# Another order of the product groups inside a planned block of an f32 encoder layer

## The chip, the cores and the metric

The kernel runs on one core of a Trainium2 chip. The metric is the time of the device in microseconds; the time before is the median of 3 runs. Matmuls run on TensorE (PE in the profile); the other engines are VectorE (DVE), ScalarE (ACT), GpSimd (POOL) and SyncE (SP), which only issues transfers here.

## The reference

One encoder layer on 256 tokens of width 2048, all in f32: a SwiGLU block, an attention mixer, a second SwiGLU block, and a gated embedding at the end, each between RMS norms. The change touches the two SwiGLU blocks only (width of the hidden layer 5632):

```python
def _swiglu(u, w_gate, w_up, w_down):
    return (jax.nn.silu(u @ w_gate) * (u @ w_up)) @ w_down

f = _swiglu(_rmsnorm(h, ffn1_pre_g[i]), ffn1_w_gate[i], ffn1_w_up[i], ffn1_w_down[i])
h = h + 0.5 * _rmsnorm(f, ffn1_post_g[i])
```

## The kernel before

**A product in three matmuls.** An f32 product is made from parts. Each operand is split into a high part, rounded to the matmul's fp32r type, and a low part, the rest: for a weight tile of two 128-row groups, `split` casts on ScalarE (line 77, `wh`) and subtracts on VectorE (line 78, `wl`). `mac` then issues three matmuls for each row group: high by high (line 104), low activations by high weights (105), high activations by low weights (106). `wh` and `wl` have 6 buffers each, so splits run at most six tiles ahead of TensorE.

**Planned blocks.** The hidden layer is worked on in 11 blocks of 512 columns for each SwiGLU. Block 0 is computed plainly. Blocks 1 to 10 of each go through `pair_product`, 20 in all, which makes the gate and up products of one block with fewer matmuls by a scheme like Strassen's. The activations of 12 of the 16 row groups form a 2 by 2 matrix (two token halves, two sets of six row groups); `s1` to `s4` are sums of its parts, made once. The weights form `ra1` and `ra2` (gate) and `rb1` and `rb2` (up), of six row groups each. `rb1` never has a tile of its own: it is added into `ra1`, and later into `rb2`, by DMAs that accumulate (`add_rows`, line 195, issued by GpSimd, in three parts of two row groups each). In between VectorE adds `rb2` into `ra1` (`add`, line 204). So each of these tiles is split, then changed in place, then split again. The products are called by their left side: a11 on the plain `ra1`; s4 on the plain `rb2`; s1 on `ra1`+`rb1`; s2 on that with `rb2` added; s3 on `rb2`+`rb1`; a12 on `ra2`; a22 on `ra1` with `ra2` added. They accumulate in four PSUM banks g0, g1, u0 and u1. ScalarE copies three of the states aside (`kept`, line 175), and VectorE combines them (line 206).

**What else lies in a block.** The last 4 of the 16 row groups aren't part of the scheme: `rest_b` multiplies two of them of the up weights with both token halves (12 matmuls, into u1 and u0), and a like step does the gate weights at the end of the block. `fill` takes one job of a list: a down step, which multiplies the previous block's hidden values with 4 row groups of the down weights (24 matmuls, line 449 on), four for each block. `run_later` transposes the previous block's hidden values and splits them into `hid_h` and `hid_l` (lines 295, 301 and 302); the down steps need them. Block 1 has `rest_first` set: its rest rows of up come at the start. In the last block two entries of the list are empty, so only two down steps lie within it.

**Order.** The loads of rest rows and down weights (`raw`, line 68, three buffers) and of `ra1`, `rb2`, `ra2` (`raw_b`, line 190, three buffers) stand in one queue on SyncE. The program is built ahead of time with the Tile layer, which sets each engine's queue and its waits from a plan; a queue is then worked through in order. In the trace TensorE's is in the order of the program, and VectorE's and ScalarE's are nearly so: where two instructions were ready at different times in the plan, they can be exchanged.

The order of TensorE's work in a block before, where `rest_first` is not set: a11, s4, transposes, s1, rest 0, down 0, s2, down 1, s3, rest 1, down 2, a12, a22, down 3, and two rest steps of gate.

Of the kernel before, what the change touches and what calls it, by code (L numbers as in the profile page):

```python
# [34 lines left out]
def encoder_layer(ctx: ExitStack, tc: tile.TileContext, a: dict, out: bass.AP):  # L35
# [35 lines left out]
    def split(raw):  # L71

        n, m = raw.shape[1:]
        wh = wpool.tile([P, 2, NB], F32R, name="wh", bufs=6)[:, :, :m]
        wl = wpool.tile([P, 2, NB], F32R, name="wl", bufs=6)[:, :, :m]
        splits[:] = [
            nc.scalar.copy(wh[:, :n], raw),  # L77
            nc.vector.tensor_tensor(wl[:, :n], raw, wh[:, :n].bitcast(F32), op=ALU.subtract),  # L78
        ]
        return [(wh[:, i], wl[:, i]) for i in range(n)]  # L80

    def load_parts(w, r0, nk, c0):

        parts = []
        for k0 in range(0, nk, 4):
            n = min(4, nk - k0)
            raw = load_rows(w, r0 + k0 * P, n, c0)
            for j in range(0, n, 2):
                parts += split(raw[:, j : min(j + 2, n)])
        return parts  # L90

    def mac(acc, xs, parts, first=False, last=False, low_last=False):


        if low_last:
            for i, ((xh, xl), (wh, wl)) in enumerate(zip(xs, parts)):
                nc.tensor.matmul(acc, xh, wh, start=first and i == 0, stop=False)
                nc.tensor.matmul(acc, xh, wl, start=False, stop=False)
            for i, ((xh, xl), (wh, wl)) in enumerate(zip(xs, parts)):
                nc.tensor.matmul(acc, xl, wh, start=False, stop=last and i == len(parts) - 1)  # L100
            return
        for i, ((xh, xl), (wh, wl)) in enumerate(zip(xs, parts)):
            lead, tail = first and i == 0, last and i == len(parts) - 1
            nc.tensor.matmul(acc, xh, wh, start=lead, stop=False, skip_group_check=True)  # L104
            nc.tensor.matmul(acc, xl, wh, start=False, stop=False, skip_group_check=True)  # L105
            nc.tensor.matmul(acc, xh, wl, start=False, stop=tail, skip_group_check=True)  # L106

    def of_tile(lhs, t):
        tok = slice(t * P, (t + 1) * P)
        return [(hi[:, tok], lo[:, tok]) for hi, lo in lhs]  # L110
# [48 lines left out]
    def run_later():  # L159
        for job in later:  # L160
            job()
        later.clear()

    def pair_product(lhs, sums, wa, ca, wb, cb, fill, rest_first):

        rows1, rows2 = ([lhs[k] for k in ks] for ks in ROWS)
        a11, a12, a22 = of_tile(rows1, 0), of_tile(rows2, 0), of_tile(rows2, 1)
        s1, s2, s3, s4 = sums

        def bank(name):  # L170
            return ps_acc.tile([P, NB], F32, name=f"pair_{name}", tag="acc")

        def kept(name, x):
            t = ffn_pool[0].tile([P, NB], F32, name=name, tag="part", bufs=3)
            nc.scalar.copy(t, x)
            return t

        def spans(j, step):
            for k0, k1 in ((0, KB), (KB, RQ)):
                for k in range(k0, k1, step):  # L180
                    yield k, min(k + step, k1)

        def weight_rows(w, j, c, k0, k1):
            r0 = ROWS[j][k0] * P
            return w[r0 : r0 + (k1 - k0) * P, c : c + NB].rearrange("(k p) n -> p k n", p=P)

        def blocks(w, j, c):
            raw = ffn_pool[0].tile([P, RQ, NB], F32, name="raw_b", bufs=3)
            for k0, k1 in spans(j, KB):
                raw_loads.append(nc.sync.dma_start(raw[:, k0:k1], weight_rows(w, j, c, k0, k1)))  # L190
            return raw

        def add_rows(raw, w, j, c):
            for k0, k1 in spans(j, 2):
                nc.gpsimd.dma_start(raw[:, k0:k1], weight_rows(w, j, c, k0, k1), accum_op=ALU.add)  # L195

        def split_rows(raw):
            return sum((split(raw[:, k : min(k + 2, RQ)]) for k in range(0, RQ, 2)), [])

        def add(out_, x, y, op=ALU.add):  # L200
            n = x.shape[1] if len(x.shape) > 2 else 0
            for k in range(0, n, 2):
                j = slice(k, min(k + 2, n))
                nc.vector.tensor_tensor(out_[:, j], x[:, j], y[:, j], op=op)  # L204
            if not n:
                nc.vector.tensor_tensor(out_, x, y, op=op)

        nk = len(lhs)
        k_rest = [(k, (nk - 2 * RQ) // 2) for k in range(2 * RQ, nk, (nk - 2 * RQ) // 2)]

        def rest(w, k, n, c, accs_, last=False):
            parts = load_parts(w, k * P, n, c)
            for t, acc, lead in accs_:
                mac(acc, of_tile(lhs[k : k + n], t), parts, first=lead, last=last)

        def rest_b(i, last):
            rest(wb, *k_rest[i], cb, [(1, u1, i == 0), (0, u0, i == 0 and rest_first)], last=last)

        u0 = u1 = None
        if rest_first:  # L220
            u0, u1 = bank("u0"), bank("u1")
            rest_b(0, False)
            run_later()
        ra1, rb2 = blocks(wa, 0, ca), blocks(wb, 1, cb)
        if rest_first:
            rest_b(1, False)
        g1 = bank("g1")
        mac(g1, a11, split_rows(ra1), first=True, last=True)
        g0_ = kept("g0_s", g1)
        add_rows(ra1, wb, 0, cb)  # L230
        u0 = u0 or bank("u0")
        mac(u0, s4, split_rows(rb2), first=not rest_first, last=rest_first)
        run_later()
        if rest_first:
            fill()
        g0 = bank("g0")
        mac(g0, s1, split_rows(ra1), first=True, last=True)
        u1_ = kept("u1_s", g0)
        add(ra1, ra1, rb2)
        add_rows(rb2, wb, 0, cb)  # L240
        if not rest_first:
            u1 = bank("u1")
            rest_b(0, False)
        fill()
        mac(g1, s2, split_rows(ra1), last=True)
        u0_ = kept("u0_s", g1)
        add(u0_, u0_, u1_, ALU.subtract)
        ra2 = blocks(wa, 1, ca)
        fill()
        mac(g1, s3, split_rows(rb2), last=True)  # L250
        if not rest_first:
            rest_b(1, True)
        add(u0_, u0, u0_, ALU.subtract)
        add(u1_, u1_, g1, ALU.subtract)
        add(u1_, u1, u1_)
        if not rest_first:
            fill()
        mac(g0, a12, split_rows(ra2), first=True)
        add(ra1, ra1, ra2)
        mac(g1, a22, split_rows(ra1))  # L260
        fill()
        for k, n in k_rest:
            rest(wa, k, n, ca, [(0, g0, False), (1, g1, False)], last=k + n == nk)
        assert len(k_rest) == 2
        add(g0_, g0, g0_)
        return (g0_, g1), (u0_, u1_)
# [159 lines left out]
    def swiglu(pool, f, ssf, res, blocks, rs, sums, w_gate, w_up, w_down, g_post):  # L426
# [35 lines left out]
        for nb in range(nbs):  # L462
            c0 = nb * NB
            if True:
                if nb > 0:
                    gate, up = pair_product(lhs, sums, w_gate, c0, w_up, c0, fill, nb == 1)
                    gs = [gated(gate[t], t) for t in range(NT)]
                else:
# [396 lines left out]
```

## Time and profile before

| | |
|---|---|
| median of 3 runs | 1961.44 us (1957.82 to 1962.08) |
| the profiled execution's own time | 1963.99 us |
| its span | 1962.2 us |
| mean granted TensorE clock | 0.994 |
| TensorE busy | 1914.2 us, 98% of the span |
| VectorE busy | 1552.7 us, 79% |
| ScalarE busy | 1119.0 us, 57% |
| read from memory | 404.79 MB, 207 GB/s over the span |

The span goes from the first to the last instruction; the time is some 2 us more. Matmuls overlap in the profile: one is shown as 0.39 us, but one starts about every 0.23 us. In a timeline row stand the start in us, the duration, the engine, the line, the operation, the tile written and the tiles read, and in brackets how long the engine was idle just before and what ended that. `raw` and `raw_b` are the weight tiles as loaded, `pair_g` and `pair_u` the banks g and u, `u_h` and `u_l` the parts of the activations, `sums_h` and `sums_l` those of s1 to s4. With several alike in a row, the start is that of the first and the duration that of all.

### The profile page before, as it was taken

To read this page: it belongs to the slowest core of one execution; us is meant where nothing else is said; L and a number is where in the kernel's file an instruction comes from. 1 tells how busy PE (TensorE), PEld (TensorE's weight loads), DVE (VectorE), ACT (ScalarE), POOL (GpSimd) and SP (SyncE) were. 2 spreads that over 40 slices of the span, in tenths; PEclk is the share of its full clock that TensorE was granted. 3 is DMA by queue.
4 is the path that set the end of the run, shared out by engine and by line. 5 is a ranking of instruction groups with operands and counts; after the bars stand their busy time and mean duration, and the time that the engine had idled before them with its cause. 6 is when DMAs were issued, how large, how long until landed. Compare 5 with 4: busy or idle time off the path is not lost.

```text
span 1962.2 us, 23327 instructions
## 1 busy us (share of the span) xinstructions
PE 1914.2 (98%) x8600; PEld 1565.5 (80%) x8600; DVE 1552.7 (79%) x1740; ACT 1119.0 (57%) x1364; POOL 173.0 (9%) x151
## 2 busy tenths in 40 slices
PE   8999999999999999999999999999999999999997
PEld 6878877787778878888888888778777877888786
DVE  7888898889888986566665588778988898889864
ACT  7665565656555654554544466555655565555653
POOL 0111001100110000000000010110011001100000
PEclk9999999999999999999999999999999999999999
DMA  9887878787877647454454578778687878776463
GB/s 348 242 226 205 259 201 223 201 261 203 228 198 242 180 154 245 153 174 155 146 194 164 179 252 226 206 185 261 204 222 196 249 206 221 203 232 183 151 235 113
DMA packets 207361, 408.40 MB, mean 208 GB/s; under 512 B 8848, under 2 KB 11920, under 8 KB 206736
## 3 DMA queue, kind: packets, MB, share of 16 engines
q1 hardware_dynamic: 174608, 344.00, 51.1%
q0 software_dynamic: 32640, 62.92, 18.2%
q8 instruction: 67, 1.10, 0.2%
q14 instruction: 46, 0.38, 0.1%
HBM read 404.79 MB, written 2.10 MB: 207 GB/s over the span
## 4 chain that ended last, share of the span: by engine, by line
PE 76%; DMA 8%; DVE 8%; issue 4%; ACT 2%; POOL 2%; POOLq 0%; DVEq 0%; ACTq 0%; SPq 0%
DMA raw_b<-in_ffn_w_up 8%; PE pair_g L105 7%; PE pair_g L104 7%; PE down L105 7%; PE pair_g L106 7%; PE down L104 7%; PE down L106 7%; DVE wl L78 3%; PE pair_u L106 3%; DVE raw_b L204 2%; PE pair_u L105 2%; PE pair_u L104 2%; ACT wh L77 2%; POOL raw_b L195 2%; PE v L106 1%
## 5 line engine op out<-in xcount | busy, mean ns | idle before, releaser
L77 ACT CAST wh<-raw 128x1024 fp32r<-128x1024 f32 (+1 forms) x453 | 469.1, 1051 | 374.2 <-PE down L105 104.6
L78 DVE TENSOR_TENSOR wl<-raw,wh 128x1024 fp32r<-128x1024 f32 (+1 forms) x453 | 543.9, 1218 | 140.2 <-ACT wh L77 126.8
L77 ACT CAST wh<-raw_b 128x1024 fp32r<-128x1024 f32 x420 | 436.5, 1050 | 334.6 <-PE down L105 130.5
L78 DVE TENSOR_TENSOR wl<-raw_b,wh 128x1024 fp32r<-128x1024 f32 x420 | 505.0, 1220 | 145.5 <-ACT wh L77 138.9
L105 PE MATMUL down<-wh,hid_l 128*128 128x512 f32 x640 | 252.7, 395 | 0.0
L104 PE MATMUL down<-wh,hid_h 128*128 128x512 f32 x640 | 251.8, 393 | 0.0
L106 PE MATMUL down<-wl,hid_h 128*128 128x512 f32 x640 | 249.8, 390 | 0.0
L195 POOL DMA_DIRECT2D raw_b<-in_ffn_w_up x120 | 146.8, 1267 | 1081.5 <-DVE wl L78 772.9
L106 PE MATMUL pair_g<-wl,u_h 128*128 128x512 f32 x520 | 202.3, 389 | 0.0
L105 PE MATMUL pair_g<-wh,u_l 128*128 128x512 f32 x520 | 202.3, 389 | 0.0
L104 PE MATMUL pair_g<-wh,u_h 128*128 128x512 f32 x520 | 202.3, 389 | 0.0
L104 PEld LDWEIGHTS down<-wh,hid_h 128*128 128x128 f32 x640 | 120.7, 189 | 28.1
L104 PE MATMUL pair_g<-wh,sums_h 128*128 128x512 f32 x360 | 143.1, 397 | 0.0
L204 DVE TENSOR_TENSOR raw_b<-raw_b 128x1024 f32<-128x1024 f32 x120 | 142.7, 1217 | 0.1
L106 PEld LDWEIGHTS down<-wl,hid_h 128*128 128x128 f32 x640 | 120.6, 188 | 27.0
L105 PE MATMUL pair_g<-wh,sums_l 128*128 128x512 f32 x360 | 141.7, 394 | 0.0
L106 PE MATMUL pair_g<-wl,sums_h 128*128 128x512 f32 x360 | 141.3, 393 | 0.0
L105 PEld LDWEIGHTS down<-wh,hid_l 128*128 128x128 f32 x640 | 120.8, 189 | 25.0
L441 DVE TENSOR_TENSOR f<-f,down 128x512 f32<-128x512 f32 x160 | 108.9, 680 | 19.0 <-PE down L106 18.1
L104 PEld LDWEIGHTS pair_g<-wh,u_h 128*128 128x128 f32 x520 | 97.6, 188 | 20.4
L105 PEld LDWEIGHTS pair_g<-wh,u_l 128*128 128x128 f32 x520 | 97.6, 188 | 20.3
L106 PEld LDWEIGHTS pair_g<-wl,u_h 128*128 128x128 f32 x520 | 97.6, 188 | 20.2
(218 smaller groups left out, 2956.8 us busy)
## 6 DMA issues: line engine op xcount, KB each, us to landing
raw<-in_ffn_w_down SPq DMA_DIRECT2D x88, 1024.0 KB, 7.4
raw_b<-in_ffn_w_up POOLq DMA_DIRECT2D x120, 512.0 KB, 10.2
raw<-in_w_qkv SPq DMA_DIRECT2D x48, 1024.0 KB, 5.1
raw_b<-in_ffn_w_gate SPq DMA_DIRECT2D x40, 1024.0 KB, 5.2
raw<-in_ffn_w_gate SPq DMA_DIRECT2D x41, 512.0 KB, 5.2
raw<-in_ffn_w_up SPq DMA_DIRECT2D x40, 512.0 KB, 6.0
raw_b<-in_ffn_w_gate SPq DMA_DIRECT2D x40, 512.0 KB, 7.9
raw_b<-in_ffn_w_up SPq DMA_DIRECT2D x20, 1024.0 KB, 5.2
```

The costliest lines, as they stand in the source:

```text
L77: nc.scalar.copy(wh[:, :n], raw),
L78: nc.vector.tensor_tensor(wl[:, :n], raw, wh[:, :n].bitcast(F32), op=ALU.subtract),
L104: nc.tensor.matmul(acc, xh, wh, start=lead, stop=False, skip_group_check=True)
L105: nc.tensor.matmul(acc, xl, wh, start=False, stop=False, skip_group_check=True)
L106: nc.tensor.matmul(acc, xh, wl, start=False, stop=tail, skip_group_check=True)
L195: nc.gpsimd.dma_start(raw[:, k0:k1], weight_rows(w, j, c, k0, k1), accum_op=ALU.add)
L204: nc.vector.tensor_tensor(out_[:, j], x[:, j], y[:, j], op=op)
L441: nc.vector.tensor_tensor(f_t, f_t, acc, op=ALU.add)
```

## The change

The groups of a block are put in another order; no instruction is added or taken out. Where `rest_first` is not set, the new order of TensorE's work is: a11, s4, transposes, rest 0, down 0, s1, rest 1, down 1, s2, down 2, s3, a12, a22, down 3, and the two rest steps of gate. So a rest step and a down step now stand between s4 and s1, another pair between s1 and s2, one down step between s2 and s3, and nothing between s3 and a12. Where `rest_first` is set, the second rest step moves from the front of the block to the place between s4 and the first down step. The `stop` marks of the accumulations move with their last matmul.

```diff
         ra1, rb2 = blocks(wa, 0, ca), blocks(wb, 1, cb)
-        if rest_first:
-            rest_b(1, False)
         g1 = bank("g1")
         mac(g1, a11, split_rows(ra1), first=True, last=True)
         g0_ = kept("g0_s", g1)
         add_rows(ra1, wb, 0, cb)
         u0 = u0 or bank("u0")
-        mac(u0, s4, split_rows(rb2), first=not rest_first, last=rest_first)
+        mac(u0, s4, split_rows(rb2), first=not rest_first)
         run_later()
-        if rest_first:
-            fill()
+        if not rest_first:
+            u1 = bank("u1")
+        rest_b(int(rest_first), rest_first)
+        fill()
         g0 = bank("g0")
         mac(g0, s1, split_rows(ra1), first=True, last=True)
         u1_ = kept("u1_s", g0)
         add(ra1, ra1, rb2)
         add_rows(rb2, wb, 0, cb)
         if not rest_first:
-            u1 = bank("u1")
-            rest_b(0, False)
+            rest_b(1, True)
         fill()
         mac(g1, s2, split_rows(ra1), last=True)
         u0_ = kept("u0_s", g1)
...
         ra2 = blocks(wa, 1, ca)
         fill()
         mac(g1, s3, split_rows(rb2), last=True)
-        if not rest_first:
-            rest_b(1, True)
         add(u0_, u0, u0_, ALU.subtract)
         add(u1_, u1_, g1, ALU.subtract)
         add(u1_, u1, u1_)
-        if not rest_first:
-            fill()
         mac(g0, a12, split_rows(ra2), first=True)
         add(ra1, ra1, ra2)
         mac(g1, a22, split_rows(ra1))
```

## The prediction

> **What bounds the kernel now.** I read the page's head, then TensorE's waits, then one steady block (374.64 to 438.80 us, the fifth planned block of the first FFN) engine by engine.
>
> ```profile
> span 1962.2 us, 23327 instructions
> ...
> PE 1914.2 (98%) x8600; PEld 1565.5 (80%) x8600; DVE 1552.7 (79%) x1740; ACT 1119.0 (57%) x1364; POOL 173.0 (9%) x151
> ...
> L77 ACT CAST wh<-raw_b 128x1024 fp32r<-128x1024 f32 x420 | 436.5, 1050 | 334.6 <-PE down L105 130.5
> ```
>
> ```profile
> PE pair_u L106 <- DVE wl L78: 25.1, 18, 2.9
> ```
>
> ```profile
> 374.64:438.80 64.16, 62.74 (x279) 51.44 (x278) 55.62 (x57) 37.55 (x40) 7.34 (x6) 1.00 0.77 218
> 129.00:140.00 11.00, 8.87 (x33) 7.10 (x33) 10.75 (x11) 4.22 (x6) 1.86 (x2) 0.84 1.07 228
> 1250.00:1262.00 12.00, 9.50 (x29) 7.64 (x30) 10.60 (x12) 4.28 (x6) 2.20 (x2) 0.72 1.05 230
> 1512.00:1520.00 8.00, 6.00 (x20) 4.66 (x20) 8.00 (x9) 3.77 (x5) 1.84 (x2) 0.79 1.06 200
> 360.00:381.00 21.00, 21.00 (x94) 17.32 (x93) 15.63 (x16) 11.19 (x12) 3.62 (x3) 1.00 0.98 271
> ```
>
> TensorE sets the end: it is busy 98% of the span. Of its idle time one line holds more than half, 25.1 us in 18 waits, and 18 is the number of planned blocks that are not rest_first (nine in each of two FFNs). The steady block (window columns: length; then busy time of PE, PEld, DVE, ACT, POOL; granted clock; DMA share; GB/s) is 64.16 long with 62.74 of matmul: 1.42 idle, which is this one wait. So only about 1.4 us in a block can be won by any order of work; more can easily be lost.
>
> ```profile
> 374.64 0.39 PE L104 MATMUL pair_g<-wh,u_h 128*128 128x512 f32 x1
> 378.72 0.39 PE L104 MATMUL pair_u<-wh,sums_h 128*128 128x512 f32 x1
> 382.85 1.04 PE L295 MATMUL tr<-ident,u_s 128*128 128x128 f32 x8
> 383.64 0.48 PE L104 MATMUL pair_g<-wh,sums_h 128*128 128x512 f32 x1
> 387.86 0.40 PE L104 MATMUL pair_u<-wh,u_h 128*128 128x512 f32 x1
> 389.91 0.50 PE L106 MATMUL pair_u<-wl,u_h 128*128 128x512 f32 x1 [1.42 <-DVE wl L78]
> 392.31 0.39 PE L104 MATMUL down<-wh,hid_h 128*128 128x512 f32 x1
> 397.80 0.39 PE L104 MATMUL pair_g<-wh,sums_h 128*128 128x512 f32 x1
> ```
>
> ```profile
> 381.81 1.05 ACT L77 CAST wh<-raw_b 128x1024 fp32r<-128x1024 f32 x1 [1.86 <-DMA raw_b<-in_ffn_w_up]
> 383.24 2.96 ACT L77 CAST wh<-raw 128x1024 fp32r<-128x1024 f32 x3
> 386.09 1.07 ACT L301 CAST hid_h<-tr 128x512 fp32r<-128x512 f32 x2
> ```
>
> ```profile
> 382.89 1.23 DVE L78 TENSOR_TENSOR wl<-raw_b,wh 128x1024 fp32r<-128x1024 f32 x1 [1.68 <-ACT wh L77]
> 384.04 3.49 DVE L204 TENSOR_TENSOR raw_b<-raw_b 128x1024 f32<-128x1024 f32 x3
> 387.44 1.28 DVE L302 TENSOR_TENSOR hid_l<-tr,hid_h 128x512 fp32r<-128x512 f32 x2
> 388.64 3.48 DVE L78 TENSOR_TENSOR wl<-raw,wh 128x1024 fp32r<-128x1024 f32 x3
> ...
> 412.07 0.68 DVE L206 TENSOR_TENSOR u_s<-u_s,pair_g 128x512 f32<-128x512 f32 x1
> ```
>
> ```profile
> 365.04 2.57 POOL L195 DMA_DIRECT2D raw_b<-in_ffn_w_up  x2 [39.71 <-DVE wl L78]
> 370.52 1.20 POOL L195 DMA_DIRECT2D raw_b<-in_ffn_w_up  x1 [2.91 <-DVE wl L78]
> 385.90 3.71 POOL L195 DMA_DIRECT2D raw_b<-in_ffn_w_up  x3 [14.18 <-DVE raw_b L204]
> ```
>
> Read backwards from 389.91. TensorE lacks the low split of the first rest rows; VectorE starts it only at 388.64, behind the last split of the summed ra1 (382.89), three adds (384.04) and the hidden splits (387.44). That queue is late because ScalarE stood until 381.81 for the last accumulating DMA into ra1, issued at 370.52: 11.3 us under way, while the DMA engines were 0.98 busy. So the wait at the rest rows is the landing of the sum, handed on through two in-order queues.
>
> **The change part by part.** Times as +x from the block's first matmul at 374.64. Nothing is added or removed: per block 12 matmuls, one split and one load for each rest step, 24 matmuls, two splits and one load for each down step, all with another neighbour. TensorE's distances are unchanged: six rows 378.72-374.64 = 4.08, down 397.80-392.31 = 5.49, a rest step 12 matmuls at down's 5.49/24 = 0.229, so 2.75 where nothing waits.
>
> *The sum gets cover.* New order: a11 +0, s4 +4.1, transposes +8.2, rest +9.0, down +11.8, s1 from +17.2 instead of +9.0. The landing at 381.81 is +7.2. The six wh buffers let the cast of s1's third tile start only when s4's third is released, about +8.2 to +8.4 (the page's row shows such releases by L105), so ScalarE no longer waits for the DMA. The rest tile is now sixth after a11's first: cast about +2, needed at +9. The wait of 25.1 us goes: **-25.1**.
>
> *The clock.* The three windows with 0.84, 0.72 and 0.79 each begin at one of the longest waits:
>
> ```profile
> 131.17 0.50 PE L106 MATMUL pair_u<-wl,u_h 128*128 128x512 f32 x1 [2.13 <-DVE wl L78]
> ...
> 132.22 0.63 PE L104 MATMUL pair_u<-wh,u_h 128*128 128x512 f32 x1
> ```
>
> ```profile
> 1252.50 0.80 PE L106 MATMUL pair_u<-wl,u_h 128*128 128x512 f32 x1 [2.93 <-DVE wl L78]
> ```
>
> ```profile
> 1514.14 0.50 PE L106 MATMUL pair_u<-wl,u_h 128*128 128x512 f32 x1 [2.00 <-DVE wl L78]
> ```
>
> Matmuls of 0.63 follow where 0.39 is usual, 1.05 us after the first of these waits has ended. The loss is 0.16 x 11 + 0.28 x 12 + 0.21 x 8 = 1.8 + 3.4 + 1.7 = 6.8 us. I take it as a consequence of the waits: **-6.8** (bounds 0 and -6.8). [...]
>
> *The hidden splits lose theirs.* This is the price. Transposes to first down matmul is 9.5 us now, 3.5 then. ScalarE: s1's third cast about +8.4 to +9.45, then hid_h (two of 0.55), the first half by +10.0. VectorE then needs 0.68 for that half of hid_l: ready at +10.7 if it is free, +11.9 if it has just begun a 1.22 us split or add. The second down matmul, which reads it, starts at +11.98. Estimate 0; bounds 0 to +0.5 a block (one split and one add ahead), 0 to +9 in all. Before, the three adds ran ahead of hid_l because they could start at 384.04 and hid_h came only at 386.09, behind three casts of raw (383.24); in the new order hid_h is ready about when s1's last low split is, and hid_l stands ahead of the adds in the program.
>
> *Loads, SP's queue.* Three raw buffers, so three loads run ahead:
>
> ```profile
> 361.94 0.37 SPq L68 DMA_DIRECT2D raw<-in_ffn_w_down  x1
> ...
> 363.30 0.37 SPq L68 DMA_DIRECT2D raw<-in_ffn_w_down  x1
> 389.92 0.37 SPq L68 DMA_DIRECT2D raw<-in_ffn_w_up  x1
> ...
> raw<-in_ffn_w_down SPq DMA_DIRECT2D x88, 1024.0 KB, 7.4
> ```
>
> The third place (363.30, 1 MB for down 1) goes to the second rest rows, half as large; 0.52 MB at 271 GB/s is 1.9 us less in front of the accumulation. Down 1's load moves from 363.30 to the release of the first rest tile, about +5; with 7.4 us it lands at +12.4, its cast is allowed at +15.9, its matmuls come at +24. Covered, 0; if the cover failed, TensorE still has 8 us. The ra2 load stands after one more raw load in the program; it waits for a buffer anyway. Value 0.
>
> *The second sum.* The adds into ra1 end about +15.3 (now +12.9), so POOL's three issues (385.90, +11.3 now) come about 3 us later and land by about +31; s3's matmuls start at +39. 0. POOL has nothing else queued in the block.
>
> *The end of the block.* Before, rest and down lay between s3 and a12, so the subtraction that reads g1 (412.07, about 0.5 us after s3's end) had 12.3 us until a22 writes g1; now it has a12's 4.1. It needs 0.68 and at most one 1.22 ahead: 0.
>
> *The rest_first block.* Its second rest step moves behind s4, so a11 comes 2.7 us sooner.
>
> ```profile
> 58.15 5.77 DVE L78 TENSOR_TENSOR wl<-raw_b,wh 128x1024 fp32r<-128x1024 f32 x5
> ...
> 59.06 0.39 PE L104 MATMUL pair_g<-wh,u_h 128*128 128x512 f32 x1
> ```
>
> In the first FFN a11's second low split ends about 59.3; TensorE would want it at 56.3 + 1.4 + 0.5 = 58.1. **+1.2**; bounds 0 to +2.7 for each of two blocks, since that queue may also move.
>
> *Sum*, against the profiled execution's 1963.99: 1963.99 - 25.1 - 6.8 + 1.2 = 1933.3. That execution is 2.55 us above the median of the runs, 1961.44; the half-rate stretches can differ between executions, and if all that difference is theirs the median loses only 4.3 of them and comes out the same. Forecast 1933.
>
> **The rivals.** [...]
>
> (b) *Part of the gain goes into a wait at the first down step*: hid_l comes with a split and an add ahead, or hid_h behind a late DMA. 0.3 to 1.0 us in 18 blocks: +5 to +18, so 1938 to 1951. For it: a margin of 0.1 to 1.3 us against in-order queues, and VectorE is 55.62 of 64.16 busy. Against: 0.68 is short and comes early in program order.
>
> (c) *Slower*: VectorE's queue keeps today's order, three adds (3.49) before hid_l. Its first half is then ready at 9.5 + 1.2 + 3.4 + 0.65 = +14.75 against +11.98: 2.75 x 18 = 50, and waits as long as these keep the half-rate stretches: 1933 + 50 + 7 = 1990. It decides from 1.75 us a block (31.9/18) on. For it: it is today's order. Against: today the adds are ready first, then they are not.
>
> (d) *No change*: the wait only moves to another split, because VectorE, not the landing, is the limit: 1961. Against: 8.5 us of VectorE idle in the block, and the new order gives each split more lead.
>
> **How the numbers follow.** Forecast 0.62, (a) 0.09, (b) 0.15, (c) 0.09, (d) 0.05. No change means within 0.2%, about 4 us, roughly what runs of this kernel differ by. Faster: 0.62 + 0.09 + 0.15 = 0.86; same 0.05; slower 0.09. The likeliest case has 1929 to 1938 (0 to +5.4 at rest_first, a few us of clock). The range adds (a) and (b): 1928 to 1951, leaving out (c) and (d), 0.14, and a little at the lower end.
>
> **What would show it.** Right: no pair_u L106 line among TensorE's waits; ScalarE's waits for the accumulating DMA near zero; block length near 62.7; granted clock 1.00 in every block; in VectorE's queue hid_l ahead of the adds. Wrong: a wait of TensorE at down L104 or L105 for hid (b, c); half-rate matmuls in blocks without waits (a); a new wait at s2 or s3 for wl, which would break the cover worked out for the sums; a wait before a22 for the subtraction; a wait above 2.7 us in a rest_first block.

## The result and the profile after

The changed kernel takes 1928.08 us (median of 5 runs, 1927.68 to 1928.54) against 1961.44 us for the kernel before (median of 5, 1957.82 to 1966.69): a ratio of 0.9831 with a 95% interval of 0.9813 to 0.9849. The forecast was 1933 with a range of 1928 to 1951. The profiled execution took 1928.43 us, 35.6 less than the profiled one of before.

The head of the page, then TensorE's longest waits, then what was left of ScalarE's waits for the accumulating DMA (in us in total, times, longest):

```profile
span 1926.7 us, 23362 instructions
...
PE 1902.8 (99%) x8600; PEld 1562.8 (81%) x8600; DVE 1554.7 (81%) x1740; ACT 1128.8 (59%) x1364; POOL 172.4 (9%) x151
```

```profile
PE gate L104 <- ACT wh L77: 6.1, 2, 5.7
PE q L97 <- ACT u_h L296: 2.2, 1, 2.2
```

```profile
ACT wh L77 <- DMA raw_b<-in_ffn_w_up: 2.9, 1, 2.9
```

The pair_u line with 25.1 us is gone, and nothing has taken its place; before, the like line of ScalarE stood at 60.4 us in 40 waits:

```profile
ACT wh L77 <- DMA raw_b<-in_ffn_w_up: 60.4, 40, 3.6
```

The same block as in the prediction, now from 365.78 us, as a window (length; busy PE, PEld, DVE, ACT, POOL; clock; DMA share; GB/s) and then as its timeline on TensorE, ScalarE, VectorE and GpSimd:

```profile
365.78:428.26 62.48, 62.48 (x280) 51.53 (x278) 55.85 (x57) 38.04 (x41) 7.31 (x6) 1.00 0.80 227
```

```profile
365.78 0.39 PE L104 MATMUL pair_g<-wh,u_h 128*128 128x512 f32 x1
...
373.99 1.04 PE L290 MATMUL tr<-ident,u_s 128*128 128x128 f32 x8
374.79 0.48 PE L104 MATMUL pair_u<-wh,u_h 128*128 128x512 f32 x1
...
377.60 0.39 PE L104 MATMUL down<-wh,hid_h 128*128 128x512 f32 x1
377.83 0.39 PE L105 MATMUL down<-wh,hid_l 128*128 128x512 f32 x1
...
383.10 0.39 PE L104 MATMUL pair_g<-wh,sums_h 128*128 128x512 f32 x1
```

```profile
373.96 1.05 ACT L77 CAST wh<-raw_b 128x1024 fp32r<-128x1024 f32 x1 [0.32 <-DVE wl L78]
374.91 1.07 ACT L296 CAST hid_h<-tr 128x512 fp32r<-128x512 f32 x2
```

```profile
374.98 1.22 DVE L204 TENSOR_TENSOR raw_b<-raw_b 128x1024 f32<-128x1024 f32 x1
376.12 1.28 DVE L297 TENSOR_TENSOR hid_l<-tr,hid_h 128x512 fp32r<-128x512 f32 x2
377.32 1.22 DVE L78 TENSOR_TENSOR wl<-raw_b,wh 128x1024 fp32r<-128x1024 f32 x1
378.45 2.36 DVE L204 TENSOR_TENSOR raw_b<-raw_b 128x1024 f32<-128x1024 f32 x2
```

```profile
361.66 1.20 POOL L195 DMA_DIRECT2D raw_b<-in_ffn_w_up  x1 [2.90 <-DVE wl L78]
```

TensorE is busy through the whole block: 62.48 of 62.48, where it was 62.74 of 64.16. The third accumulating DMA is issued at -4.1 as before, and lands 9.1 us later, at +4.9, where it was 11.2 us and +7.1; s1 now starts at +17.3. ScalarE casts the third tile of the sum at +8.2 without a wait for a DMA, and VectorE makes hid_l at +10.3, behind one of the three adds and ahead of the other two. TensorE needs its first half by +12.05 (377.83).

### The profile page after: what moved, and what is told of

The parts are those of the page before. It is cut to its first block, busy times and chain, and to the rows that moved or that the text cites. A ratio compares the mean times of both kernels' runs of the same rounds, so it can differ in the third digit from the quotient of the medians.

```text
span 1926.7 us, 23362 instructions
## 1 busy us (share of the span) xinstructions
PE 1902.8 (99%) x8600; PEld 1562.8 (81%) x8600; DVE 1554.7 (81%) x1740; ACT 1128.8 (59%) x1364; POOL 172.4 (9%) x151
## 3 DMA queue, kind: packets, MB, share of 16 engines
HBM read 404.79 MB, written 2.10 MB: 211 GB/s over the span
## 4 chain that ended last, share of the span: by engine, by line
PE 95%; DVE 2%; ACT 1%; issue 1%; DMA 1%; POOL 0%; SPq 0%; DVEq 0%; POOLq 0%; ACTq 0%
PE pair_g L105 10%; PE pair_g L104 10%; PE pair_g L106 10%; PE down L105 8%; PE down L104 8%; PE down L106 8%; PE pair_u L104 3%; PE pair_u L105 3%; PE pair_u L106 3%; PE v L106 2%; PE v L105 2%; PE v L104 2%; PE mo L106 1%; PE mo L104 1%; PE mo L105 1%; PE tr L290 1%
## 5 line engine op out<-in xcount | busy, mean ns | idle before, releaser
L104 PE MATMUL down<-wh,hid_h 128*128 128x512 f32 x640 | 251.3, 393 | 0.0
L104 PE MATMUL pair_g<-wh,u_h 128*128 128x512 f32 x520 | 202.5, 389 | 0.0
L104 PEld LDWEIGHTS down<-wh,hid_h 128*128 128x128 f32 x640 | 120.2, 188 | 27.9
L104 PE MATMUL pair_g<-wh,sums_h 128*128 128x512 f32 x360 | 141.7, 394 | 0.0
L104 PEld LDWEIGHTS pair_g<-wh,u_h 128*128 128x128 f32 x520 | 97.6, 188 | 20.4
```

## The experiments

Ratios are to the kernel before, run beside each variant on the same chip; intervals are 95%.

**Without the first sum.** Is the landing of the sum the cause at all?

```diff
-        add_rows(ra1, wb, 0, cb)
```

> The order of before; the three accumulating DMAs into ra1 are left out, so the products s1 and s2 lack rb1's share. Theory (the landing of that sum is the cause, handed on through two queues): ScalarE has nothing to wait for, VectorE's queue runs about 3 us earlier at the rest rows, the 18 waits of TensorE go, and with them the half-rate stretches in the blocks: 1927 to 1931 us. Rival (VectorE's own work is the limit): the low split of the rest rows stays behind three adds and the hidden splits, the waits stay at 1 us or more in a block: 1950 to 1961.

Measured: 1928.42 us, ratio 0.9841 (0.9822 to 0.9859). TensorE's order is still that of before, yet the time is that of the changed kernel. VectorE's work is the same, so it isn't the limit, and rival (d) falls. The run also reads 31 MB less (373.33 for 404.79), so by itself it doesn't tell the landing from the traffic; the next run, which keeps the traffic, does.

**The rest step alone.**

```diff
         if rest_first:
             fill()
+        else:
+            u1 = bank("u1")
+            rest_b(0, False)
         g0 = bank("g0")
...
-        if not rest_first:
-            u1 = bank("u1")
-            rest_b(0, False)
         fill()
```

> Only the first rest step moves ahead of s1; the down step stays behind s1. Theory: s1 then starts at +11.8 instead of +9.0 and the next raw tile whose low split TensorE needs is down 0's, at +16.4; VectorE's queue (last split of the sum to about +9.6, three adds to +13.0, hidden to +14.2, down 0's first low split to +15.4) is just in time: no wait above 0.3 us in a block, 1928 to 1934 us. Rival (both steps are needed as cover): a wait of 0.5 to 1.4 us in a block at down 0, 1940 to 1958.

Measured: 1931.16 us (four runs, 1930.33 to 1938.98), ratio 0.9869 (0.9839 to 0.9899). Some 2.75 us of other matmuls ahead of s1 are cover enough in a steady block. The sum lands at +7.1 in this trace as in that of before (medians over 16 blocks, the second to the ninth planned one of each FFN, counted from a11's first matmul), so it is the cover that takes the waits away, not an earlier landing. The waits that it has and the changed kernel hasn't (0.35, 0.72 and 0.26 us) are in the last block of each FFN (see the next but one).

**The down step alone.**

```diff
-        if rest_first:
-            fill()
+        fill()
         g0 = bank("g0")
...
-        fill()
+        if rest_first:
+            fill()
         mac(g1, s2, split_rows(ra1), last=True)
```

> Only the first down step moves ahead of s1; the rest step stays behind s1. The sum has cover (s1 at +14.5). Theory: the price is the hidden values: the first down step comes straight after the transposes, whose first half ends near +8.7; hid_h and hid_l need 0.55 + 0.68 and places in two queues, so TensorE waits 1.0 to 2.2 us (and loses about 0.25 more) for hid in each of 18 blocks: 1950 to 1975 us with some half-rate stretches. Rival (hid was never tight, either step covers alike): 1928 to 1932.

Measured: 1938.21 us, ratio 0.9892 (0.9873 to 0.9910): slower than the change by 10 us, but less than the theory had it. There is no wait for hid; instead a steady block of the first FFN is 62.8 us long, 0.3 more than the 62.48 of the change (see the late transposes below). The rest is in the last block of each FFN: four waits of 0.7 to 1.0 us and a half-rate stretch (granted clock 0.79 from 1756 to 1764 us).

**The first pair alone**, with the second half of the block as before.

```diff
-        if rest_first:
-            fill()
+        if not rest_first:
+            u1 = bank("u1")
+            rest_b(0, False)
+        fill()
         g0 = bank("g0")
...
-        if not rest_first:
-            u1 = bank("u1")
-            rest_b(0, False)
-        fill()
+        if rest_first:
+            fill()
         mac(g1, s2, split_rows(ra1), last=True)
```

> Rest 0 and down 0 move ahead of s1 as in the change; s2 then follows s1 directly, and the second half of the block (down 1, s3, rest 1, down 2) stays as before. Theory: the gain is in the first pair alone; the adds are done before s2's casts are allowed, and the second sum lands some 4 us before s3 needs it: no wait, 1927 to 1931 us. Rival (the pairs further on carry part of the gain): a wait at s2 or s3 of 0.5 us or more in a block, 1940 or above.

Measured: 1931.25 us, ratio 0.9856 (0.9838 to 0.9875). Nearly the whole gain is in the first pair, but 3 us are not. In this kernel's trace the waits left in planned blocks are three, all in the last block of an FFN, at the second rest step. That block has only two down steps, and none of them lies between s2 and s3 here; one of the waits is this line of TensorE's waits between 640 and 645 us:

```profile
PE pair_u L106 <- DVE wl L78: 0.5, 1, 0.5
```

The kernel before has the same wait (658 us in its timeline), and the change, which puts that rest step between s1 and s2 and a down step between s2 and s3, has none:

```profile
657.99 0.50 PE L106 MATMUL pair_u<-wl,u_h 128*128 128x512 f32 x1 [0.61 <-DVE wl L78]
```

Its cause is the other sum, the one into rb2. In the kernel before ScalarE waits for its landing just ahead of the casts of the rest tile, and the low split that TensorE needs is the first of the three that follow:

```profile
654.49 1.05 ACT L77 CAST wh<-raw_b 128x1024 fp32r<-128x1024 f32 x1 [2.18 <-DMA raw_b<-in_ffn_w_up]
```

```profile
656.72 3.49 DVE L78 TENSOR_TENSOR wl<-raw,wh 128x1024 fp32r<-128x1024 f32 x3
```

The landing itself is at 654.39; in the second FFN it is at 1780.88, again 0.1 us ahead of the cast. The run without the first sum keeps a wait at this place (0.26 us), so it is not the first sum's. In the other blocks a down step of 5.5 us lies between s2 and s3.

**Late transposes**: the changed order, with the transposes behind the rest step.

```diff
-        run_later()
         if not rest_first:
             u1 = bank("u1")
         rest_b(int(rest_first), rest_first)
+        run_later()
         fill()
```

> The changed order, but the transposes of the hidden values come after the rest step, straight ahead of the first down step. The cover of the sum is that of the change. Theory: TensorE waits for hid, since transposes, hid_h and hid_l now lie one after the other in front of the down step: 0.9 to 2.0 us plus about 0.25 in each of 18 blocks, 1945 to 1970 us. Rival (the margin of the hidden splits is wide): 1928 to 1931.

Measured: 1933.90 us, ratio 0.9870 (0.9854 to 0.9886): 5.8 us slower than the change, between the two expectations. The price I had named did not come as a wait, because TensorE's queue was not in the order of the program. Its timeline after the transposes:

```profile
378.56 0.48 PE L104 MATMUL pair_g<-wh,sums_h 128*128 128x512 f32 x1
378.87 0.39 PE L105 MATMUL pair_g<-wh,sums_l 128*128 128x512 f32 x1
379.31 0.50 PE L104 MATMUL down<-wh,hid_h 128*128 128x512 f32 x1
379.65 0.40 PE L106 MATMUL pair_g<-wl,sums_h 128*128 128x512 f32 x1
379.89 0.39 PE L104 MATMUL pair_g<-wh,sums_h 128*128 128x512 f32 x1
```

The plan has put matmuls of s1 ahead of and between the first ones of the down step. What is left are two starts that come 0.44 and 0.34 us after the one before instead of 0.23, some 0.3 us a block. Over 18 blocks that is 5.4 of the 5.8 us. So the hidden splits do have a price when the transposes come late, but a smaller one than a plain wait. The trace with the down step alone has the same two starts in its steady blocks.

**The adds later.** TensorE's order of before; only VectorE's queue is changed.

```diff
-        add(ra1, ra1, rb2)
-        add_rows(rb2, wb, 0, cb)
         if not rest_first:
             u1 = bank("u1")
             rest_b(0, False)
+        add(ra1, ra1, rb2)
+        add_rows(rb2, wb, 0, cb)
```

> TensorE's order is that of before. Only the three adds of rb2 into ra1, with the accumulating DMAs that follow them, stand after the first rest step in the program, so that VectorE can split the rest rows ahead of the adds. Theory (the late landing reaches TensorE only through VectorE's queue): the low split of the rest rows moves up by the 3.5 us of the adds and the wait of about 1.4 us goes: 1928 to 1933 us. Rival (the landing itself holds TensorE, so only cover on TensorE helps): the waits stay, 1955 to 1962. Should the adds still come first in VectorE's queue, the time says nothing and the queue's order is to be read.

Measured: 1943.37 us, ratio 0.9923 (0.9899 to 0.9947). The queue did change: the low split of the rest rows now stands ahead of the adds (377.88), and down 0's two come behind them (383.63):

```profile
377.88 1.23 DVE L78 TENSOR_TENSOR wl<-raw,wh 128x1024 fp32r<-128x1024 f32 x1 [0.21 <-ACT wh L77]
379.03 2.35 DVE L204 TENSOR_TENSOR raw_b<-raw_b 128x1024 f32<-128x1024 f32 x2
381.30 1.28 DVE L302 TENSOR_TENSOR hid_l<-tr,hid_h 128x512 fp32r<-128x512 f32 x2
382.50 1.22 DVE L204 TENSOR_TENSOR raw_b<-raw_b 128x1024 f32<-128x1024 f32 x1
383.63 2.35 DVE L78 TENSOR_TENSOR wl<-raw,wh 128x1024 fp32r<-128x1024 f32 x2
```

```profile
PE down L106 <- DVE wl L78: 5.3, 9, 1.1
```

The wait at the rest rows is gone from the steady blocks, and part of it has moved on to those splits in down 0. So the lateness does reach TensorE through VectorE's queue, but reordering that queue wins only about half; cover on TensorE takes it away.

**A later third DMA**, to make the waits longer and see whether the half-rate stretches follow waits of some 2 us or need longer ones: one, six and nine small powers on GpSimd (each 1.03 us) between the second and the third accumulating DMA, in the order of before. They read a low tile of a11 (`parts1[4][1]`); their values are used nowhere.

```diff
             for k0, k1 in spans(j, 2):
+                if after is not None and k0 == KB:
+                    nc.gpsimd.tensor_tensor(pad, after, mhalf[:, :4], op=ALU.pow)
                 nc.gpsimd.dma_start(raw[:, k0:k1], weight_rows(w, j, c, k0, k1), accum_op=ALU.add)
...
-        add_rows(ra1, wb, 0, cb)
+        add_rows(ra1, wb, 0, cb, after=None if rest_first else parts1[4][1][:, :4].bitcast(F32))
```

> The order of before, with one small power on GpSimd (about 1.5 us as in the line of r in the trace, its value used nowhere) between the second and the third accumulating DMA into ra1, outside the rest_first blocks: the sum lands about 1.5 us later. Theory of the landing: the wait at the rest rows grows by 1.5 us in 16 blocks, +24 us to about 1983. Theory of the clock (waits of 2 us and more bring half-rate stretches): nearly every such block now has a wait of 2.5 to 3.5 us and many get a stretch of 3.4 us at half rate, another 1.7 us each, so 1990 to 2010 and a granted clock of 0.975 or less. [...]

> The order of before, with six of the small powers (1.03 us each) between the second and the third accumulating DMA into ra1, so that it is issued 6 us later, past the time in which the DMA engines are full. Theory of the landing: it then lands 1 to 3 us later than in the order of before, the wait at the rest rows grows to 2.5 to 4.5 us in 16 blocks: +16 to +48 us, 1976 to 2008. Theory of the clock: with waits of 2 us and more, half or more of the 16 blocks show a stretch of 3.4 us at half rate (another 1.7 us each, in the upper half of that range), the granted clock falls to 0.985 or less. [...]

> As with six, but nine powers, another 3.1 us. Both theories of the clock expect stretches here, since the wait is 4 to 7 us: the time is 48 us above that with six for the waits (16 x 3.1), with a half-rate stretch in nearly every block, 2030 to 2070. It shows whether time then follows the issue of the third DMA one to one, as the theory of the landing has it.

Measured: 1963.67 (1.0007, 0.9992 to 1.0022), 1963.61 (1.0007, 0.9990 to 1.0025) and 1968.87 us (1.0043, 1.0030 to 1.0056). The expectations failed, in two ways. With six and nine, only the first power stands ahead of the DMA in GpSimd's queue (here with six), the others behind it, so the delay was never more than one power. The issue comes at -3.38, 0.74 us later than in the kernel before:

```profile
370.28 1.03 POOL L198 TENSOR_TENSOR pad<-wl,mhalf 128x4 f32<-128x4 f32 x1 [2.65 <-DVE wl L79]
371.28 1.23 POOL L199 DMA_DIRECT2D raw_b<-in_ffn_w_up  x1
372.07 7.06 POOL L198 TENSOR_TENSOR pad<-wl,mhalf 128x4 f32<-128x4 f32 x5
```

And that delay did not make the sum land later: it lands at +6.9 with one power and at +7.0 with six, against +7.1 (the same medians as above), and TensorE's waits come to 23.2 and 24.1 us. So the landing did not follow the issue here. That the DMA engines, 0.98 busy from 360 to 381 us in the kernel before, set it instead is the author's guess and was not tried. The times can't be compared as finely: in these traces a block of the second FFN is some 0.4 us shorter without its wait than in the kernel before and the changed one, about 4 us in all, for a reason that is not known; and the profiled executions with one and with six powers are the fastest of their ten. With nine the powers held a low tile, VectorE waited for its place (13.9 us in 7 waits in the trace), and TensorE's waits rose:

```profile
PE pair_u L107 <- DVE wl L79: 32.8, 20, 2.2
```

Whether the stretches need longer waits was not told apart in the way planned: no wait at the rest rows came above 2.2 us, so no run shows what one of 4 to 7 us does. What these runs say of the clock stands below.

**The rest_first blocks** in the order of before, the rest as changed, and beside it the changed kernel again.

```diff
+        if rest_first:
+            rest_b(1, False)
         g1 = bank("g1")
...
-        rest_b(int(rest_first), rest_first)
+            rest_b(0, False)
         fill()
```

> The changed kernel, but the two rest_first blocks keep the order of before. If the charge of the prediction were right (+1.2 us for the new order there), this is 1.2 us faster than the changed kernel, about 1927. Theory after the trace (no wait in either order): the same within 0.6 us, 1927.5 to 1928.7.

> The changed kernel itself, beside the one with the old rest_first blocks: 1927.7 to 1928.6 us.

Measured: 1927.99 us (0.9830, 0.9815 to 0.9845) and 1927.76 us (0.9829, 0.9814 to 0.9844). No difference: that part of the change does nothing to the time.

## Why the prediction was right, and where its terms were off

The measured median lies only 0.08 us inside the lower end of the range, and the changed kernel measured again beside the rest_first variant came to 1927.76, just below it. The mechanism was right; that its sizes still fell within the range was luck.

**The sum gets cover: right.** The waits went with the sum, as the run without it shows, and they went with the cover alone where the sum landed as late as before (+7.1). That the delay is handed on by VectorE's queue, worked through in order, shows in the block of before: the rest tile's cast had ended at 384.29 (383.24 + 1.05), but its low split began at 388.64, behind the adds and the hidden splits. The earlier landing came too: +4.9 instead of +7.1 in the block shown, some 2 us where 1.9 was worked out, though no run tests that the smaller load ahead is its reason.

**Where the 18 waits lay: wrong in part.** I read 18 as one wait in each of nine blocks of each FFN. Sixteen lie so, in the second to the ninth planned block, at the first rest step. In the last block of each FFN the listed wait is at the second rest step (0.61 at 657.99 above, and 0.30 in the second FFN), and what it waits for is the landing of the second sum, not the first: no down step covers it there. The prediction asked of the second sum only whether the new order would make a wait, and found 0. The change removes this one too, by its second part, which I had costed at nothing.

**What a wait costs: mis-sized.** This is the term behind most of the 4.9 us between 1933 and the measured median; the rest_first charge of 1.2 is the other. I priced a wait by its idle time, 1.42 us in the steady block. But the block went from 64.16 to 62.48, by 1.68. These lines of before show why:

```profile
388.10 0.39 PE L105 MATMUL pair_u<-wh,u_l 128*128 128x512 f32 x1
389.91 0.50 PE L106 MATMUL pair_u<-wl,u_h 128*128 128x512 f32 x1 [1.42 <-DVE wl L78]
390.24 0.39 PE L104 MATMUL pair_u<-wh,u_h 128*128 128x512 f32 x1
```

The idle time counts from the end of a matmul, 0.39 after its start, while the next would have started 0.23 after it: 389.91 - 388.10 - 0.23 = 1.58. The first matmul after the wait then takes 0.33 to the next start, another 0.10. Together 1.68, or 0.26 more than the idle time; 16 times that is 4.2 us. The blocks of the second FFN are 62.95 us long in the changed kernel, with no idle time either; without its wait a block of the kernel before is as long there, so this is no cost of the change.

**The clock: -6.8, borne out, though not as a rule.** The changed kernel has no half-rate stretch in a planned block, nor have the runs without the sum, with the rest step alone, with the first pair alone and with the late transposes. In the first stretch of the kernel before, from 132.2 to 135.3 us, the granted clock is 0.50 and matmuls start about 0.43 us apart, not 0.23. Where there are stretches, each comes at a wait: three in the kernel before, one each with the adds later, with nine powers and with the down step alone. In the first and the last of these three the stretch begins at two shorter waits whose ends are 1.45 us apart (1.42 and 0.72 with the adds later); with the down step alone it is seen by the 0.63 of the last line:

```profile
1756.25 0.50 PE L104 MATMUL pair_u<-wh,u_h 128*128 128x512 f32 x1 [0.95 <-ACT wh L77]
...
1757.70 0.50 PE L106 MATMUL pair_u<-wl,u_h 128*128 128x512 f32 x1 [0.72 <-DVE wl L78]
...
1758.57 0.63 PE L106 MATMUL pair_u<-wl,u_h 128*128 128x512 f32 x1
```

But such a wait in a planned block does not always bring one: the kernel before has five waits between 1.92 and 2.93 us and a stretch at three of them (2.13, 2.93 and 2.00). In the block from 1318 to 1382 us the clock stayed at 1.00 with this wait:

```profile
1320.64 0.50 PE L106 MATMUL pair_u<-wl,u_h 128*128 128x512 f32 x1 [2.23 <-DVE wl L78]
```

```profile
1318.00:1382.00 64.00, 61.77 (x273) 50.32 (x272) 55.53 (x57) 37.37 (x40) 7.10 (x7) 1.00 0.78 222
```

With nine powers nine waits were between 1.89 and 2.16 us, and one stretch followed. The runs say the same: without waits they lie within 0.9 us of each other (1927.68 to 1928.54); with six powers they go from 1954.62 us at a granted clock of 0.999 to 1968.59 at 0.994. So this is a cost that comes and goes between executions, and the median of before had its share. That the clock loss would stay without the waits, which had 0.09 as (a), is out for the time; that only the waits make the difference is a strong coincidence of these runs, not a test with longer waits.

**The hidden splits: right, with a margin of one microsecond.** Their first half was expected between +10.7 and +11.9 and needed by +11.98. It was done about +11.0 (376.12 + 0.68) and needed at +12.05. One add stood ahead, not three; the prediction's sign, hid_l ahead of all the adds, held only for two of them, and the margin took up the third. What I did not see is that a late hid would be met by a change in TensorE's own queue: with the transposes late it costs 0.3 us a block, the lowest price of (b), where (c) had 2.75 for a plain wait.

**Loads, the second sum, the end of the block: right at 0.** TensorE has no wait in any planned block.

**The rest_first block: wrong.** +1.2 was charged, 0 measured (1927.99 against 1927.76). The step that failed took a11's low splits at their place of before, where all but the first stood behind the hidden splits:

```profile
56.71 1.29 DVE L302 TENSOR_TENSOR hid_l<-tr,hid_h 128x512 fp32r<-128x512 f32 x2 [0.70 <-ACT hid_h L301]
```

In the new order VectorE goes on with them from 51.63, before the hidden splits, as two lines of its timeline and one of TensorE's (a11's first matmul) show:

```profile
51.63 2.35 DVE L78 TENSOR_TENSOR wl<-raw_b,wh 128x1024 fp32r<-128x1024 f32 x2
...
58.33 1.28 DVE L297 TENSOR_TENSOR hid_l<-tr,hid_h 128x512 fp32r<-128x512 f32 x2
```

```profile
56.94 0.48 PE L104 MATMUL pair_g<-wh,u_h 128*128 128x512 f32 x1
```

The sum then closes: of 35.6 us between the profiled executions, 25.1 are idle time in waits, about 4.2 what idle time doesn't show, and up to 6.8 the clock, together 36.1; the waits at gate L104, outside the planned blocks, are 0.7 longer after (6.1 for 5.4).

## What to carry to other kernels

Price a wait of a pipelined engine by the distance of two starts, not by its idle time: here 1.68 us for a shown 1.42. Between a tile's use and the use of the same tile changed in place by a DMA, put work that doesn't depend on it, and do it for every such sum, in the last block too, where the list of filling work runs short (here 0.61 and 0.30 us of wait in the kernel before); here 2.75 us of it were enough at the first sum, and the work that is used as cover must itself not be fed by something just made (0.3 us a block with the transposes late). And read a queue's order from the trace for each variant: a plan may exchange ready work even on the engine that sets the end, so a wait argued from program order can come out as something smaller (0.3 us a block here, for the 0.9 to 2.0 expected).

## What the runs showed of the hardware that I had not expected

A stretch of half clock can follow a wait of TensorE of 2.00 us, or two shorter ones that end 1.45 us apart, and it need not: in the planned blocks of all traces it followed 4 of the 16 waits of 1.89 us or more. One wait outside them does it far oftener. Each of the 13 traces has 2.2 us ahead of the attention's first q product, behind transposes, and in 11 of them a half-rate stretch begins within 2.3 us of its end; why there is open. In the kernel before:

```profile
721.90 0.50 PE L97 MATMUL q<-wh,u_h 128*128 128x512 f32 x1 [2.20 <-ACT u_h L301]
...
722.72 0.63 PE L98 MATMUL q<-wl,u_h 128*128 128x512 f32 x1
```

An accumulating DMA issued 0.74 us later landed no later (+6.9 and +7.0 against +7.1), in a stretch where the DMA engines were 0.98 busy in the kernel before (360 to 381 us).
